# Two-layer backbone on one Trainium2 core: a PSUM copy held ahead of a weight cast in three feed-forward pairs, and one modulation dot instead of two before the token norm

## The chip, the cores and the metric

The program runs on one core of one Trainium2 chip. The metric is the device time of one execution in microseconds (us). The median of three runs of the kernel before is 1104.1 us, the lowest 1103.16, the highest 1105.3.

## What is computed

A residual stream of 512 latent tokens and 256 context tokens, 1024 features wide, passes through two layers. The first layer mixes tokens by latent attention and a short convolution, the second by a two-dimensional Fourier transform. Each layer ends in a SwiGLU feed-forward block. What the change touches is this block and the norm ahead of the Fourier transform:

```python
x = x + g1 * out_l
x = x + g2 * swiglu(rmsnorm(x, norm2_g[i]) * (1 + sc2) + sh2, ffn_w1[i], ffn_w3[i], ffn_w2[i])

def swiglu(h, w1, w3, w2):
    return (jax.nn.silu(h @ w1) * (h @ w3)) @ w2
```

The modulation vectors (`sh`, `sc`, `g`) come from `jax.nn.silu(c) @ ada_w[i] + ada_b[i]`, with 6144 outputs per layer.

## The kernel before, in words

**Arithmetic.** A product of 32-bit precision is made of three passes on TensorE (PE): each operand is split into a high and a low part, and high times high, low times high and high times low are added up in one PSUM bank. The split of a raw weight tile (128x1024) is one cast on ScalarE (ACT), whose name ends in `h`, and one subtraction on VectorE (DVE), whose name ends in `l` (`wsplit`, L151, and `split`, L142). Nearly every instruction is recorded at L92, the helper through which the engines are called, so it is followed by the names of its tiles.

**The feed-forward block.** `ffn` computes the up projections `h @ w1` and `h @ w3` for 22 blocks of 128 hidden features. The first 4 blocks of layer 0 and the first 6 of layer 1 are computed plainly (`up`); the others in pairs `p` of two blocks by a scheme with seven products instead of eight (`up_pair`, L1227). A product is 24 matmuls of 256 columns. Four PSUM banks belong to a pair: `ba`, `bb`, `be`, `bf`, in the trace `s_a`, `s_b`, `s_e`, `s_f`. The products come in this order:

- `11` into `ba`; then ACT copies `ba` into `bb` (L1258, in the trace `s_b<-s_a`);
- `s1` into `be`; then ACT copies `be` into an SBUF tile (L1261, in the trace `c<-s_e`);
- `s2`, added to `ba`, which may start when the copy `s_b<-s_a` has read `ba` and the weights `w_s2h` and `w_s2l` are split;
- `s4`, added to `be`; `s3`, added to `ba`; `12`, added to `bb`; `22`, added to `bf`.

Where the banks are still unused (`new`, L1234), a matmul of 512 columns first fills `bb` and `bf` (`fill_bank`). That is so in three pairs: pairs 2 and 3 of layer 0 and pair 3 of layer 1. After the pairs the down projection `w2` follows, whose weights are named `w_0` to `w_7`.

**Dots.** A modulation output is a dot of a row tile of `ada_w` with `silu(c)` on DVE (`dot`, L195; in the trace `junk<-ada,csil`, 128x1024). Dots are work in the background: `step(it, n)` emits the next `n` of them at chosen places. In layer 0 their row tiles have two buffers (`adap.tile(..., bufs=2)`, L1345), so the load of a row tile waits until the dot two places ahead of it has read its buffer.

**Order.** A scheduler orders each engine's instructions ahead of time, and each engine runs its list in that order. An instruction that passes through `tc.keep_in_program_order` keeps the program's order among the others that do; the dots do so, and the ones that `nc.ordered(True, ...)` covers. All loads are issued by SP, in one list too.

**The token norm.** Ahead of the Fourier transform, eight matmuls sum the squares of each token (`nm1st`), a short chain on DVE and ACT makes the reciprocal root (`rtok`), and four products `v` are scaled by it, split into `v1h` and `v1l` and go into the products `z`. Two dots are emitted ahead of that chain (L1426), and further ones between the splits (L1439).

Of the kernel before, what the change touches and what calls it, by code (L numbers as in the profile page):

```python
# [10 lines left out]
F32R = mybir.dt.float32r  # L11
# [6 lines left out]
P = 128  # L18
D = 1024
# [90 lines left out]
def backbone(ctx: ExitStack, tc: tile.TileContext, a, out):  # L110
    nc = Core(tc)
    PSUM = bass.MemoryType.PSUM

    def pool(name, bufs=1, side="left"):
        return tc.alloc_tile_pool(name=name, bufs=bufs, side=side, reuse_waits="tile")
# [10 lines left out]
    def ps2(name):  # L126
        return ps["pool"].tile([P, 2, 512], F32, tag="s2", name=name, bufs=3)
# [6 lines left out]
    def load(src, name, slots=None):  # L134
        t = slots(name) if slots else rawp.tile([P, src.shape[1]], F32, tag="raw", name=name)
        nc.sync.dma_start(out=t, in_=src)
        return t

    def f(ap):
        return ap.bitcast(F32)  # L140

    def split(hi, lo, src, eng=None):  # L142
        nc.scalar.copy(hi, src)
        (eng or nc.vector).tensor_sub(lo, src, f(hi))
# [6 lines left out]
    def wsplit(wpool, src, name, r_=None, eng=None):  # L151
        if r_ is None:
            r_ = load(src, name)
        n = r_.shape[1]
        hi = wpool.tile([P, n], F32R, tag="whi", name=name + "h")
        lo = wpool.tile([P, n], F32R, tag="wlo", name=name + "l")
        split(hi, lo, r_, eng)
        return hi, lo

    def step(it, n=1):  # L160
        for _ in range(n):
            next(it, None)
# [50 lines left out]
    def ada_chunk(l, chunk, by_pool=False, slots=None):  # L213

        m, sums = chunk * 8, []
        for i in range(8):
            w = load(a["ada"][l, m + i], f"ada{l}_{m + i}", slots)
            if by_pool:
                for n, _ in enumerate(dot_pool(w, csil)):
                    if n == LAG and sums:  # L220
                        total(*sums.pop())
                    yield
                sums.append((mod[:, l, m + i:m + i + 1], w))
            else:
                dot(mod[:, l, m + i:m + i + 1], w, csil)
                yield
        if sums:
            total(*sums.pop())
        nc.vector.tensor_add(mod[:, l, m:m + 8], mod[:, l, m:m + 8], col(C_AB + 48 * l + m, 8))
        if chunk in (1, 4):  # L230
            which = 0 if chunk == 1 else 1
            scale_cols(amod[:, l, which, :], mod[:, l, m:m + 8], col((C_N1, C_N2)[which] + 8 * l, 8))
# [249 lines left out]
    for n, k in enumerate(order):  # L482
# [20 lines left out]
        wh, wl = qw[k]  # L503
# [22 lines left out]
    def gain_split(src, g, hi, lo):  # L526
        nc.scalar.activation(hi, src, AF.Identity, scale=g)
        nc.vector.scalar_tensor_tensor(lo, src, g, f(hi), op0=ALU.mult, op1=ALU.subtract)
# [13 lines left out]
    def weight():  # L542

        taken.append(stream[len(taken)])
        return taken[-1]
# [85 lines left out]
    for c in range(3):  # L631
        w = weight()
# [147 lines left out]
    pin = tc.keep_in_program_order  # L780
# [169 lines left out]
    for i in range(NI - 3):  # L950
        h, t = divmod(i, 4)
# [60 lines left out]
    ring = pool("ring", RING, side="right")  # L1012
# [14 lines left out]
    def bank(o, i, t0, t1):  # L1027

        if t1 - t0 == T:
            return o[:, i, :]  # L1030
        return o[t0 // (t1 - t0)][:, 0, i * (t1 - t0):(i + 1) * (t1 - t0)]
# [120 lines left out]
    def cell(name):  # L1152

        return gfn.tile([P, 4, HT], F32, tag="c", name=name, bufs=4)

    def gate(sl, up_, hi, lo):

        if up_ is not None:
            nc.vector.tensor_mul(sl, up_, sl)
        split(hi, lo, sl)  # L1160
# [37 lines left out]
    def ffn(l, nf_, after, filler, nfill, first=None, first_out=lambda: None):  # L1198
# [28 lines left out]
        def up_pair(p, bank, g_):  # L1227

            def got(b):
                return load(a["wu"][l, p, b], f"wu{l}_{p}_{b}")  # L1230

            x_, y_, w_, z_ = (got(b) for b in range(4))
            bb, bf, ba, be = (bank(f"s{l}_{p}_{nm}") for nm in "bfae")
            new = len(used) <= 8  # L1234

            def fill_bank(o):

                if new:
                    nc.tensor.matmul(o, hh[:, KT - 1, 0:P], hh[:, KT - 1, :], start=True, stop=True)

            cf = gfn.tile([P, 2, 2, HT], F32, tag="c", name=f"c{l}_{p}", bufs=4)
            quads = [cf[:, i].rearrange("p w n -> p (w n)") for i in range(2)]

            def product(o, raw, block, start):

                wh, wl = wsplit(ring, None, f"w{l}_{p}_{block}", raw)
                rh, rl = bl[block]
                for i in range(2):
                    for k in range(4):
                        s = slice((4 * i + k) * P, (4 * i + k + 1) * P)  # L1250
                        d = o[:, i * HT:(i + 1) * HT]
                        for n, (wv, rv) in enumerate(((wh, rh), (wh, rl), (wl, rh))):
                            nc.tensor.matmul(d, wv[:, s], rv[:, k, :], start=start and i == k == n == 0,
                                             stop=(i == 1 and k == 3 and n == 2), skip_group_check=True)

            product(ba, x_, "11", True)
            fill_bank(bb)
            nc.scalar.copy(bb, ba)  # L1258
            nc.vector.tensor_sub(x_, y_, x_)
            product(be, x_, "s1", True)  # L1260
            nc.scalar.copy(quads[1], be)  # L1261
            nc.vector.tensor_sub(x_, w_, x_)
            product(ba, x_, "s2", False)
            fill_bank(bf)
            nc.scalar.copy(quads[0], ba)
            product(be, w_, "s4", False)
            nc.vector.tensor_add(quads[0], be, quads[0])
            nc.vector.tensor_sub(y_, w_, y_)
            product(ba, y_, "s3", False)
            nc.scalar.copy(bf, ba)  # L1270
            nc.vector.tensor_add(quads[1], ba, quads[1])
            product(bb, z_, "12", False)
            nc.vector.tensor_sub(x_, z_, x_)
            product(bf, x_, "22", False)
            gs = [[w[:, (2 * p + j) % 8, :].rearrange("p (i n) -> p i n", i=2) for w in g_] for j in range(2)]
            sl, up_ = cf[:, :, 0, :], cf[:, :, 1, :]
            nc.scalar.activation(sl, sl, AF.Silu)
            gate(sl, up_, *gs[1])
            sl = cell(f"sl{l}_{p}")[:, 0:2, :]
            for i, o in enumerate((bb, bf)):  # L1280
                nc.scalar.activation(sl[:, i, :], o[:, 0:HT], AF.Silu)
                nc.vector.tensor_mul(sl[:, i, :], o[:, HT:T], sl[:, i, :])
            gate(sl, None, *gs[0])
# [7 lines left out]
        for c, (c0, c1) in enumerate(CHUNKS):  # L1291
# [23 lines left out]
            for p in range(max(c0, NSTD[l]) // 2, c1 // 2):  # L1315
                up_pair(p, bank8, g_)
                step(it, nfill[0][c])
# [79 lines left out]
    def first(o, t, gs):  # L1397
        s = slice(t * P, (t + 1) * P)
        for g in gs:
            for j in range(2):  # L1400
                mm3(o[:, g // 2, (g % 2) * 256:(g % 2) * 256 + 256], [gained[nm][:, 2 * g + j, s] for nm in ("hi", "lo")],
                    (dft[0][:, j, :], dft[1][:, j, :]), j == 0, j == 1)
# [20 lines left out]
        first(v1_ps[t], t, range(3))  # L1423
    rtok = small("rtok", 4)
    late_dots = ada_chunk(1, 5, slots=lambda nm: cell(nm).rearrange("p k n -> p (k n)"))
    step(late_dots, 2)  # L1426
    nc.ordered(True, "vector", "scalar")
    gained["sums"].mean(0, T, D, rtok)
    rsqrt(rtok, rtok, 4, "rtok")
    for t in range(4):  # L1430
        if t < 2:
            first(v1_ps[t], t, (3,))
            o = v1_ps[t]
        else:
            o = ps2(f"v1_{t}")
            first(o, t, range(4))
        ov = o.rearrange("p two n -> p (two n)")
        gain_split(ov, rtok[:, t:t + 1], v1h[:, t].rearrange("p g c -> p (g c)"), v1l[:, t].rearrange("p g c -> p (g c)"))
        step(late_dots, (0, 0, 1, 2)[t])  # L1439
    wn = rawp.tile([4, D], F32, tag="raw", name="wn")  # L1440
    nc.sync.dma_start(out=wn, in_=a["wnyq"])
    wnh, wnl = (ring1.tile([P, D], F32R, tag=tag, name=f"wn_{tag}")[0:4] for tag in ("whi", "wlo"))
# [4 lines left out]
    for j in range(9):  # L1447
# [4 lines left out]
        for t in range(4):  # L1452
            if j == 8:
                w = (v1h[:, t, :, 128], v1l[:, t, :, 128])
            else:
                c0 = 0 if j < 4 else 128
                w = (v1h[:, t, j % 4, c0:c0 + 128], v1l[:, t, j % 4, c0:c0 + 128])
            mm3(zo, w, (tab[0][:, t, :], tab[1][:, t, :]), t == 0, t == 3 and tab is st_)
        for i in range(0 if tab is st_ else 2):
            if j < 4:  # L1460
                w = [w[:, i, 0:128] for w in dft], [w[:, 2 * j + i, :] for w in (pairs_h, pairs_l)]
            else:
                w = [w[:, i:KT:2, 0] for w in (pairs_h, pairs_l)], [w[:, KT + i, :] for w in (pairs_h, pairs_l)]
# [43 lines left out]
    for m in range(KT):  # L1507
# [4 lines left out]
        wh, wl = wfs[m]  # L1512
# [186 lines left out]
```

## Time and profile before

| | |
|---|---|
| median of 3 runs | 1104.1 us (1103.16 to 1105.3) |
| the profiled execution | 1105.53 us, of it 1103.5 us span |
| mean granted TensorE clock | 0.989 |
| PE busy | 97% of the span |
| DVE, ACT, POOL busy | 80%, 48%, 13% |

The span reaches from the first to the last instruction; some 2 us of the execution lie around it. Times of single instructions count from the span's start. PE is busy nearly throughout, so what matters are the few places in which it waits. [...]

### The profile page before, as it was taken

The page shows a single profiled execution, that of the slowest core. Times are in us where ns is not written, and L with a number is a line of the kernel's source. Part 1 is how long each engine was busy: PE and PEld are TensorE (multiplying, and loading weights), DVE is VectorE, ACT ScalarE, POOL GpSimd, SP SyncE. Part 2 cuts the span into 40 slices and gives each one's busy share as a digit, 9 for nine tenths or more (in the row PEclk, how much of TensorE's full clock was granted, in tenths as well). Part 3 has the DMA queues.
Part 4 walks back from the last instruction along what each step waited for, and adds up shares of the span by engine and source line. Part 5 has one row for each costly group of instructions (what it writes and reads, how often), then busy time and mean ns, then how long its engine had stood idle before and what let it go on. Part 6 is the DMA issues. An engine that isn't in the chain of part 4 may idle for free.

```text
span 1103.5 us, 17128 instructions
## 1 busy us (share of the span) xinstructions
PE 1066.9 (97%) x6704; PEld 950.2 (86%) x6704; DVE 877.4 (80%) x1282; ACT 528.6 (48%) x826; POOL 144.9 (13%) x160
## 2 busy tenths in 40 slices
PE   8799998999989999999999999999999999999998
PEld 7577886888888898899989988988888899989997
DVE  6988869998789897889678989898895577745862
ACT  5354456988445452256415564363543155523540
POOL 3811237775000000000000000011000000000000
PEclk8999999999999999999999999998999999999999
DMA  7778640111661357643674573313334124422231
GB/s 257 248 277 293 216 154 17 39 39 39 229 211 58 122 191 260 206 156 116 190 221 142 162 269 134 114 41 108 122 92 157 39 96 134 134 96 73 71 96 67
DMA packets 45528, 156.95 MB, mean 142 GB/s; under 512 B 5252, under 2 KB 6276, under 8 KB 45320
## 3 DMA queue, kind: packets, MB, share of 16 engines
q1 hardware_dynamic: 45448, 155.87, 43.2%
q8 instruction: 52, 0.85, 0.3%
q14 instruction: 28, 0.23, 0.1%
HBM read 153.75 MB, written 2.10 MB: 141 GB/s over the span
## 4 chain that ended last, share of the span: by engine, by line
PE 78%; DVE 15%; ACT 3%; issue 3%; DMA 1%; POOL 1%; SPq 0%; ACTq 0%; DVEq 0%; POOLq 0%
PE f L92 24%; PE s_a L92 12%; PE s_e L92 8%; PE s_f L92 4%; PE s_b L92 4%; PE s_ps L92 4%; PE o L92 3%; DVE junk L92 2%; PE t_ps L92 2%; PE pv_ps L92 2%; PE ob L92 2%; PE fo L92 2%; PE ou L92 2%; PE oc L92 1%; PE f_third L92 1%
## 5 line engine op out<-in xcount | busy, mean ns | idle before, releaser
L92 DVE SCALAR_TENSOR_TENSOR junk<-ada,csil 128x1024 bf16<-128x1024 f32 x88 | 113.3, 1288 | 14.6 <-DMA ada<-in_ada 13.9
L92 DVE SCALAR_TENSOR_TENSOR x<-f,mod,x 128x512 f32<-128x512 f32 (+1 forms) x50 | 36.4, 728 | 65.2 <-PE f L92 65.1
L92 DVE TENSOR_TENSOR wu<-wu,wu 128x1024 f32<-128x1024 f32 x68 | 83.1, 1222 | 1.2
L92 POOL TENSOR_TENSOR w<-w,mod 128x1024 f32<-128x1024 f32 x4 | 7.9, 1972 | 474.9 <-DVE w_0l L92 456.1
L92 PE MATMUL s_a<-sh,w_s2h 128*128 128x256 f32 x136 | 39.1, 288 | 2.3 <-ACT s_b L92 2.3
L92 PE MATMUL s_a<-sh,w_s2l 128*128 128x256 f32 x136 | 39.2, 288 | 0.1
L92 PE MATMUL s_a<-sl,w_s2h 128*128 128x256 f32 x136 | 39.0, 287 | 0.0
L92 PE MATMUL s_e<-sh,w_s1l 128*128 128x256 f32 x136 | 38.4, 283 | 0.0
L92 PE MATMUL s_e<-sh,w_s1h 128*128 128x256 f32 x136 | 38.4, 282 | 0.0
L92 PE MATMUL s_e<-sl,w_s1h 128*128 128x256 f32 x136 | 38.4, 282 | 0.0
L92 PE MATMUL s_a<-sh,w_s3l 128*128 128x256 f32 x136 | 38.4, 282 | 0.0
L92 PE MATMUL s_a<-sh,w_s3h 128*128 128x256 f32 x136 | 38.3, 282 | 0.0
L92 PE MATMUL s_a<-sl,w_s3h 128*128 128x256 f32 x136 | 38.3, 282 | 0.0
L92 ACT CAST w_11h<-wu 128x1024 fp32r<-128x1024 f32 x17 | 17.8, 1050 | 41.4 <-PE f L92 18.0
L92 DVE TENSOR_TENSOR w_22l<-wu,w_22h 128x1024 fp32r<-128x1024 f32 x17 | 20.8, 1225 | 20.1 <-ACT w_22h L92 20.1
L92 ACT CAST w_s2h<-wu 128x1024 fp32r<-128x1024 f32 x17 | 17.8, 1050 | 39.4 <-DVE wu L92 26.8
L92 DVE TENSOR_TENSOR ptl<-t_ps,pth 128x384 fp32r<-128x384 f32 x62 | 31.4, 547 | 3.2 <-ACT pth L92 3.0
L92 POOL TENSOR_SCALAR p<-p,m 128x768 f32<-128x768 f32 x32 | 29.0, 908 | 24.1 <-DVE m L92 20.9
L92 DVE TENSOR_REDUCE m<-s_ps 128x1 f32<-128x768 f32 x32 | 30.3, 948 | 0.6 <-PE s_ps L92 0.5
L92 ACT CAST w_s1h<-wu 128x1024 fp32r<-128x1024 f32 x17 | 17.9, 1051 | 26.8 <-DVE wu L92 17.2
L92 ACT ACTIVATE p<-s_ps,m 128x768 f32<-128x768 f32 x32 | 29.2, 913 | 0.8 <-DVE m L92 0.8
L92 ACT CAST pth<-t_ps 128x384 fp32r<-128x384 f32 x62 | 26.6, 479 | 5.5 <-PE t_ps L92 5.1
(1011 smaller groups left out, 4161.9 us busy)
## 6 DMA issues: line engine op xcount, KB each, us to landing
ada<-in_ada SPq DMA_DIRECT2D x96, 512.0 KB, 4.5
wu<-in_wu SPq DMA_DIRECT2D x68, 512.0 KB, 4.1
w<-in_w SPq DMA_DIRECT2D x52, 512.0 KB, 4.3
adac<-in_ada SPq DMA_DIRECT2D x16, 512.0 KB, 5.8
wc<-in_wconv SPq DMA_DIRECT2D x12, 512.0 KB, 5.1
w<-in_w SPq DMA_DIRECT2D x16, 384.0 KB, 3.8
wo<-in_wo SPq DMA_DIRECT2D x8, 512.0 KB, 4.2
wf<-in_wf SPq DMA_DIRECT2D x8, 512.0 KB, 4.4
```

The source lines that it names most:

```text
L92: ins = fn(*args, **kw)
```

## The change

In the three pairs whose banks are new, the copy `s_b<-s_a` and the cast that makes `w_s2h` are both kept in program order, so that the scheduler may no longer put the cast ahead of the copy. To that end the split of a product's weights is written out. Ahead of the token norm one dot is emitted instead of two; the other is emitted behind the second `v1l`.

```diff
+            pin = False
+
+            def keep(ins):
+                return tc.keep_in_program_order(ins) if pin else ins
+
             def product(o, raw, block, start):
 
-                wh, wl = wsplit(ring, None, f"w{l}_{p}_{block}", raw)
+                wh = ring.tile([P, D], F32R, tag="whi", name=f"w{l}_{p}_{block}h")
+                wl = ring.tile([P, D], F32R, tag="wlo", name=f"w{l}_{p}_{block}l")
+                keep(nc.scalar.copy(wh, raw))
+                nc.vector.tensor_sub(wl, raw, f(wh))
                 rh, rl = bl[block]
...
             product(ba, x_, "11", True)
             fill_bank(bb)
-            nc.scalar.copy(bb, ba)
+            pin = new
+            keep(nc.scalar.copy(bb, ba))
             nc.vector.tensor_sub(x_, y_, x_)
+            pin = False
             product(be, x_, "s1", True)
             nc.scalar.copy(quads[1], be)
             nc.vector.tensor_sub(x_, w_, x_)
+            pin = new
             product(ba, x_, "s2", False)
+            pin = False
...
-    step(late_dots, 2)
+    step(late_dots)
...
-        step(late_dots, (0, 0, 1, 2)[t])
+        step(late_dots, (0, 1, 1, 2)[t])
```

The first place is ACT's list in pair 2 of layer 0 (`w_2` and `s_2` are that pair's weights and banks, `f_3`, `sl_3`, `gh_0` belong to the block before it). Rows with a minus stand in the order before, rows with a plus in the new one.

```order
 L92 CAST nf0hi<-u_s_3513 128x4x256
+L92 ACTIVATE sl_3_3670<-f_3_0_3618 128x512
+L92 CAST gh_0_3313<-sl_3_3670 128x512
+L92 COPY s_2_b<-s_2_a 128x512
+L92 COPY c_2_3694<-s_2_e 128x512
 L92 CAST w_2_s2h<-wu_2_0_3682 128x1024
-L92 ACTIVATE sl_3_3670<-f_3_0_3618 128x512
 L92 CAST w_2_s4h<-wu_2_2_3686 128x1024
-L92 CAST gh_0_3313<-sl_3_3670 128x512
 L92 CAST w_2_s3h<-wu_2_1_3684 128x1024
-L92 COPY s_2_b<-s_2_a 128x512
 L92 CAST w_2_12h<-wu_2_3_3688 128x1024
```

Not only the copy `s_b<-s_a` but also the copy `c<-s_e` now stands ahead of the cast of `w_s2h`; the casts of `w_s4h` and `w_s3h` stand behind it as before. In pair 3 of layer 0 and pair 3 of layer 1 the two copies and the casts stand in the same order.

The second place is DVE's list in pair 3 of layer 0, where three dots stood between the low parts of the weights (`w_3_s2l` and so on); `ada_42` to `ada_45` are the row tiles of the dots.

```order
 L92 TENSOR_TENSOR gl_0_3314<-sl_2_3907,gh_0_3313 128x512
 L92 SCALAR_TENSOR_TENSOR junk,mod<-ada_42_3914,csil 128x1024
+L92 SCALAR_TENSOR_TENSOR junk,mod<-ada_43_3917,csil 128x1024
+L92 SCALAR_TENSOR_TENSOR junk,mod<-ada_44_3920,csil 128x1024
+L92 TENSOR_TENSOR w_3_s2l<-wu_3_0_3926,w_3_s2h 128x1024
+L92 SCALAR_TENSOR_TENSOR junk,mod<-ada_45_3923,csil 128x1024
+L92 TENSOR_TENSOR w_3_s4l<-wu_3_2_3930,w_3_s4h 128x1024
 L92 TENSOR_TENSOR w_3_s3l<-wu_3_1_3928,w_3_s3h 128x1024
-L92 SCALAR_TENSOR_TENSOR junk,mod<-ada_43_3917,csil 128x1024
```

`w_3_s2l` and `w_3_s4l`, which stood ahead of the dot of `ada_42`, now stand behind the dots of `ada_44` and `ada_45`.

The third place is DVE's list at the token norm (`nm1st` are the summed squares).

```order
 L92 SCALAR_TENSOR_TENSOR amod<-mod,cols 128x8
 L92 SCALAR_TENSOR_TENSOR junk,mod<-ada_40_6769,csil 128x1024
-L92 SCALAR_TENSOR_TENSOR junk,mod<-ada_41_6772,csil 128x1024
-L92 TENSOR_SCALAR rtok<-nm1st_6775 128x4
+L92 TENSOR_SCALAR rtok<-nm1st_6772 128x4
 L92 RECIPROCAL rtoks<-rtoks 128x4
```

The dot of `ada_41` leaves its place ahead of `rtok`; it now stands between the second and the third `v1l`.

## Rows read from the trace of the kernel before

**Rows 1.** The page: busy time, share of the span and count of each engine.

```profile
PE 1066.9 (97%) x6704; PEld 950.2 (86%) x6704; DVE 877.4 (80%) x1282; ACT 528.6 (48%) x826; POOL 144.9 (13%) x160
```

**Rows 2.** Busy time by windows: length, busy time (instructions) by engine, granted clock, DMA share, GB/s.

```profile
354.00:687.00 333.00, 332.01 (x2211) 303.24 (x2211) 284.80 (x367) 148.45 (x200) 0.00 (x0) 1.00 0.56 180
```

**Rows 3.** Timeline of PE, pair 3 of layer 1: start, duration, instruction, idle before.

```profile
820.27 0.28 PE L92 MATMUL s_e<-sh,w_s1l 128*128 128x256 f32 x1
822.83 0.39 PE L92 MATMUL s_a<-sh,w_s2h 128*128 128x256 f32 x1 [2.27 <-ACT s_b L92]
...
827.54 0.28 PE L92 MATMUL s_e<-nf1hi,w_s4h 128*128 128x256 f32 x1
...
830.26 0.28 PE L92 MATMUL s_a<-sh,w_s3h 128*128 128x256 f32 x1
```

**Rows 4.** Timeline of ACT, pair 3 of layer 1.

```profile
818.84 1.05 ACT L92 CAST w_s2h<-wu 128x1024 fp32r<-128x1024 f32 x1 [3.25 <-DVE wu L92]
...
822.20 0.58 ACT L92 COPY s_b<-s_a 128x512 f32<-128x512 f32 x1
```

**Rows 5.** Busy time by windows, token norm and pair 3 of layer 1.

```profile
686.00:690.00 4.00, 1.86 (x13) 1.56 (x13) 2.69 (x5) 3.13 (x3) 0.00 (x0) 1.00 0.53 210
820.60:822.80 2.20, 0.00 (x0) 0.00 (x0) 2.20 (x4) 2.20 (x5) 0.00 (x0) 1.00 0.00 0
...
824.10:827.50 3.40, 3.40 (x17) 3.37 (x16) 2.19 (x2) 0.43 (x2) 0.00 (x0) 0.50 0.67 211
827.60:830.00 2.40, 2.40 (x23) 2.40 (x22) 1.23 (x1) 1.14 (x2) 0.00 (x0) 1.00 0.76 266
```

**Rows 6.** Timeline of ACT, pair 2 of layer 0.

```profile
373.65 1.05 ACT L92 CAST w_s2h<-wu 128x1024 fp32r<-128x1024 f32 x1 [3.62 <-PE f L92]
...
380.44 1.05 ACT L92 CAST w_12h<-wu 128x1024 fp32r<-128x1024 f32 x1 [1.56 <-issue]
381.40 0.58 ACT L92 COPY c<-s_e 128x512 f32<-128x512 f32 x1
```

**Rows 7.** Timeline of PE, pairs 2 and 3 of layer 0.

```profile
380.19 0.28 PE L92 MATMUL s_e<-sh,w_s1l 128*128 128x256 f32 x1
...
383.43 0.28 PE L92 MATMUL s_e<-nf0hi,w_s4h 128*128 128x256 f32 x1
...
386.15 0.29 PE L92 MATMUL s_a<-sh,w_s3h 128*128 128x256 f32 x1
...
400.59 0.29 PE L92 MATMUL s_a<-sh,w_s2h 128*128 128x256 f32 x1
...
406.42 0.29 PE L92 MATMUL s_a<-sh,w_s3h 128*128 128x256 f32 x1
```

**Rows 8.** Timeline of DVE, pairs 2 and 3 of layer 0.

```profile
374.73 1.23 DVE L92 TENSOR_TENSOR w_s2l<-wu,w_s2h 128x1024 fp32r<-128x1024 f32 x1 [2.11 <-ACT w_s2h L92]
...
386.42 0.69 DVE L92 TENSOR_TENSOR c<-s_e,c 128x512 f32<-128x512 f32 x1 [0.79 <-PE s_e L92]
...
399.28 1.22 DVE L92 SCALAR_TENSOR_TENSOR junk<-ada,csil 128x1024 bf16<-128x1024 f32 x1
...
405.27 1.23 DVE L92 SCALAR_TENSOR_TENSOR junk<-ada,csil 128x1024 bf16<-128x1024 f32 x1 [0.20 <-DMA ada<-in_ada]
```

**Rows 9.** Timeline of SP's list, pair 3 of layer 0: issues of loads.

```profile
400.54 0.33 SPq L136 DMA_DIRECT2D ada<-in_ada  x1
```

**Rows 10.** All 96 loads of `ada` tiles on SP's list, from issue to landing.

```profile
DMA to landing us min/median/max: 3.3/4.5/8.7
```

**Rows 11.** Timeline of DVE at the token norm.

```profile
684.06 1.22 DVE L92 SCALAR_TENSOR_TENSOR junk<-ada,csil 128x1024 bf16<-128x1024 f32 x1
...
685.21 0.16 DVE L92 TENSOR_SCALAR rtok<-nm1st 128x4 f32<-128x4 f32 x1
```

**Rows 12.** Timeline of PE at the token norm.

```profile
687.67 0.39 PE L92 MATMUL z<-tab_sh,v1h 128*128 128x258 f32 x1 [1.57 <-ACT v1h L92]
...
688.99 0.39 PE L92 MATMUL v<-tab_sh,nm1hi 128*128 128x256 f32 x1 [0.57 <-DVE v1l L92]
```

## The prediction

> **What bounds the kernel now.** I read the busy shares first: PE is busy for 97% of the span, the next engine (DVE) for 80% [rows 1]. So the kernel is a chain of matmuls, and a change pays or costs where PE waits. A row of windows then shows how few waits there are in the part in question: from the last plain block of layer 0 to the token norm PE is busy for 332.01 of 333.00 us [rows 2]. Two conclusions follow. The two layer-0 pairs that the change touches have no wait to remove. And a wait that is put there is not made good later: nothing behind it is idle that could take it up.
>
> The timeline of PE shows the waits at the other two places. In pair 3 of layer 1 the last matmul of `s1` starts at 820.27 and the first of `s2` at 822.83, after 2.27 us idle, ended by the copy `s_b<-s_a` [rows 3]. ACT shows why: it cast `w_s2h` at 818.84 and three more tiles before it came to the copy at 822.20 [rows 4]. [...] At the token norm PE waits 1.57 us and a little later 0.57 [rows 12].
>
> **The change part by part.**
>
> *Order on ACT.* The change asks for the copy ahead of the cast of `w_s2h`. The new order puts the copy `c<-s_e` ahead of it as well, and that copy reads the bank that `s1` writes; it cannot start before `s1` ends. So the weights of `s2`, which before were cast some 6 us ahead (373.65, against the end of `s1` at 380.47 [rows 6, 7]), now begin to be made when PE already wants them. From the end of `s1` the path is: copy 0.58 (the next instruction on ACT starts about 0.09 before the end of the one ahead: 380.44 + 1.05 against 381.40), cast 1.05 [rows 6], low part on DVE 1.23, which starts 0.03 after the cast ends [rows 8], and 0.1 for three handovers: 0.04 + 0.49 + 1.05 + 0.03 + 1.23 + 0.05 = 2.9 us. PE is not wholly idle in this time: the new order gives it the fill of `bf` and two matmuls each of `s2` and `s4`. What is left for PE then is 22 matmuls of `s2` and 22 of `s4`. Before, 24 of `s4` took 386.15 - 383.43 = 2.72, and `s2` with the fill (as long as two) took 383.43 - 380.31 = 3.12, so 0.12 each [rows 7]; `s2` started 0.12 after the last matmul of `s1`. 22 and 22 make 2.64 + 2.49 = 5.1.
>
> *Pair 2 of layer 0.* `s1` ends at 380.47; +2.9 is 383.4; +5.1 is 388.5, against 386.15, where `s3` started before [rows 7]. **+2.4 us.** Below 2.1 it can't go: that would need the three steps of the path to be shorter than their rows. The weights of `s3` and after are made while PE works on `s2` and `s4`, and stay ahead.
>
> *Pair 3 of layer 0.* Here DVE comes on top. `w_s2l` now stands behind the dots of `ada_42`, `ada_43` and `ada_44`, and the tile of `ada_44` is loaded into the buffer that the dot of `ada_42` frees. In the trace before, that dot ran at 399.28, SP issued the load at 400.54, and the dot of `ada_44` could start at 405.27, ended by the load [rows 8, 9]: 4.7 us after the buffer was free. It hurt nobody then, since `w_s2l` and `w_s4l` had gone ahead. When does the dot of `ada_42` run now? DVE's sum `c<-s_e` of pair 2 ran at 386.42 and comes 2.4 later, 388.8. From there to the dot took 12.9 us of nearly full DVE work; two low parts leave this stretch (2 x 1.2) and one enters (`w_22l`, which stood ahead): 11.6 at most, less what DVE waited in it. I take 400.2 for the dot, 401.5 for the issue, 406.2 for the dot of `ada_44`, 407.4 for `w_s2l`, 408.6 for PE. 5.1 later is 413.7, against 406.42 [rows 7]: +7.3, of which 2.4 came from pair 2. **+4.9 us.** The dot of `ada_45` and `w_s4l` end near 411, just when PE is through with `s2`; half a microsecond may be lost there. The bounds come from the load: the 96 loads of such tiles take 3.3 to 8.7, median 4.5 [rows 10], which makes +3.5 to about +9.
>
> *The clock in pair 3.* Its wait is some 4.6 us but for four matmuls, twice the 2.27 that brought the clock down in layer 1 [rows 3, 5]. So I charge one fall, **+1.6 us**; bounds 0 and two falls, 3.2.
>
> *Pair 3 of layer 1.* The 2.27 wait for `s_b<-s_a` goes, but the same path as in layer 0 takes its place: `s1` ends at 820.55, +2.9 is 823.5, +5.1 is 828.6, if the clock stays at 1.00. Before, `s3` started at 830.26 [rows 3]. **-1.7 us**, or 0 if the clock falls as before. So a stall is exchanged for one about as long, and what is won is only its fall of the clock.
>
> *Token norm.* One dot of 1.22 leaves the path to `rtok` [rows 11], PE's 1.57 wait behind it shrinks by as much [rows 12], and the 0.57 wait moves along. The dot returns ahead of the third `v1l`, which then is ready no earlier than before, and some of the gain may be lost there. **-1.0 us**, bounds 0 and -1.6. All else (the split written out, the order of `z`) issues the same instructions.
>
> **Sum:** 2.4 + 4.9 + 1.6 - 1.7 - 1.0 = +6.2 us. The profiled execution took 1105.53 (span 1103.5), so the sum gives 1111.7 for one like it; it lay 1.4 above the median of the runs. On the median it is 1104.1 + 6.2 = **1110.3 us**. About 0.2% (2.2 us) is what a measurement of this kernel can tell from no change.
>
> **The rivals.**
>
> *The clock falls in the other two pairs too.* In the forecast pair 2 of layer 0 and pair 3 of layer 1 keep it. Their waits are about 1.4 and 0.6 us with two matmuls between; the nearest row, 1.57 and 0.57 with four between, kept 1.00 [rows 5, 12], but 2.27 in one piece did not. Each fall adds 1.6: 1111.9 with one, 1113.5 with both. [...]
>
> *The load of `ada_44` lands in time.* Then pair 3 costs 2.3 like pair 2 and its clock stays: 2.4 + 2.3 - 1.7 - 1.0 = +2.0, that is 1106.1: not slower by what can be told. It decides at 404.7, where the cast of `w_s2h` ends; the tile would have to land by 403.4, some 2 us after its buffer is free. Against it: no load took under 3.3 [rows 10]. For it: only that DVE may reach the first dot earlier than I count.
>
> *The copy doesn't hold the cast,* because it need not wait for the whole of `s1`. Then pair 2 loses nothing, and in layer 1 `s2` follows `s1` at once: `s3` at 820.43 + 3.12 + 2.72 = 826.2, 4.1 ahead of before. The dots in pair 3 still stand in the way: `w_s2l` comes 2.4 earlier than I count, PE at 406.2, `s3` at 411.3, +4.9. Sum 4.9 - 4.1 - 1.0 = -0.2: 1103.9, no change, or 1105.5 with a fall of the clock in pair 3. Against it: `c<-s_e` started at 381.40, after the end of `s1` at 380.47 [rows 6, 7]. Only this and the load in time together make it faster: 1099.
>
> *More is late in pair 3:* a slow load, or `w_s4l` later than `s2` ends: 1 to 4 us more, 1111 to 1114 and, with another fall of the clock, 1115.
>
> **How the numbers follow.** Forecast 0.53; more falls of the clock 0.28; more late in pair 3 0.07; load in time 0.06; copy not in the way 0.04; both of these 0.02. Low end: the forecast with a load of 3.3 (-1.4), no fall in pair 3 (-1.6) and a little more from the norm (-0.3): 1107.0. High end: both further falls and a load that is 1.5 late: 1115.0. This leaves out the last three cases and the tails. Slower by over 0.2% takes the first three: 0.88; within 0.2% the load in time and the copy: 0.10; faster both: 0.02.
>
> **What would show it.** In the timeline of ACT the cast of `w_s2h` starts right behind `c<-s_e`, about 0.5 us after the end of `s1`, in all three pairs. On PE the third matmul of `s2` waits for `w_s2l`, in pair 3 of layer 0 for 2 us and more, with the dot of `ada_44` ended by its load just ahead. The clock is 0.50 for a stretch after that. In layer 1 the wait for `s_b` is gone. At the token norm PE waits about 0.4 us for `v1h`. I am wrong if PE runs on from `s1` to `s2` in layer 0, or if the stretch between those pairs and the token norm turns out shorter than before by what the pairs lost.

## The result, and the profile after

The changed kernel took **1114.95 us** (median of 4 runs, 1114.27 to 1115.49); the kernel before, run beside it, 1104.70 (4 runs, 1103.16 to 1108.28). The ratio is **1.0094, 95% interval 1.0072 to 1.0115**: slower, as forecast, but by some 10 us where the sum was 6.2. A second set of runs (`after_again`, below) gave 1.0069, 1.0055 to 1.0083, which is 8 us. Beside the experiments the kernel before ran 74 times more (1101.4 to 1108.88), in three sets with medians of 1105.2, 1106.2 and 1105.9, so the base of 1104.1 on which the forecast stood was 1 to 2 us low.

The profiled execution of the change took 1115.09 us (span 1113.2), that of before 1105.53 (span 1103.5): +9.6. First the page of the change: the busy times and the two groups of PE that wait.

```profile
PE 1072.7 (96%) x6704; PEld 953.5 (86%) x6704; DVE 877.0 (79%) x1282; ACT 528.7 (47%) x826; POOL 144.5 (13%) x160
...
L92 PE MATMUL s_a<-sh,w_s2h 128*128 128x256 f32 x136 | 40.3, 296 | 4.3 <-ACT w_s2h L92 4.3
L92 PE MATMUL s_a<-sh,w_s2l 128*128 128x256 f32 x136 | 40.5, 298 | 1.1 <-DVE w_s2l L92 1.1
```

PE is busy for 5.8 us more than before [rows 1] with as many instructions: matmuls ran longer, at a mean granted clock of 0.983 against 0.989. And it waits 4.3 us for `w_s2h`, three waits of some 1.4, one for each pair that the change touches. The means on the page say the same of `s2`: its matmuls with `sh` and `w_s2h` took 296 ns on average, those of `s3` with `w_s3h` 282.

To find where the time went I compared the starts of the same matmuls, the last of `s1` and the first of `s3`, in both traces. Timeline of PE of the change; in square brackets stands the idle time just before a matmul, and what ended it:

```profile
382.70 0.28 PE L92 MATMUL s_e<-sh,w_s1l 128*128 128x256 f32 x1
384.66 0.39 PE L92 MATMUL s_a<-sh,w_s2h 128*128 128x256 f32 x1 [1.44 <-ACT w_s2h L92]
385.60 0.39 PE L92 MATMUL s_e<-nf0hi,w_s4h 128*128 128x256 f32 x1 [0.44 <-ACT w_s4h L92]
385.95 0.42 PE L92 MATMUL s_a<-sh,w_s2l 128*128 128x256 f32 x1
...
392.66 0.28 PE L92 MATMUL s_a<-sh,w_s3h 128*128 128x256 f32 x1
...
406.98 0.28 PE L92 MATMUL s_e<-sh,w_s1l 128*128 128x256 f32 x1
408.88 0.39 PE L92 MATMUL s_a<-sh,w_s2h 128*128 128x256 f32 x1 [1.39 <-ACT w_s2h L92]
409.82 0.46 PE L92 MATMUL s_e<-nf0hi,w_s4h 128*128 128x256 f32 x1 [0.44 <-ACT w_s4h L92]
411.62 0.58 PE L92 MATMUL s_a<-sh,w_s2l 128*128 128x256 f32 x1 [1.11 <-DVE w_s2l L92]
...
419.16 0.28 PE L92 MATMUL s_a<-sh,w_s3h 128*128 128x256 f32 x1
...
833.60 0.39 PE L92 MATMUL s_a<-sh,w_s2h 128*128 128x256 f32 x1 [1.45 <-ACT w_s2h L92]
834.54 0.39 PE L92 MATMUL s_e<-nf1hi,w_s4h 128*128 128x256 f32 x1 [0.44 <-ACT w_s4h L92]
...
840.10 0.28 PE L92 MATMUL s_a<-sh,w_s3h 128*128 128x256 f32 x1
```

One line more of pair 3 before, beside [rows 7]:

```profile
400.47 0.28 PE L92 MATMUL s_e<-sh,w_s1l 128*128 128x256 f32 x1
```

The three first matmuls of `s3` stand 6.51, 12.74 and 9.84 us behind those of before [rows 7, 3]. What a pair costs is read here and below from the last matmul of `s1` to the first of `s3`: 9.96 us in pair 2 and 12.18 in pair 3, against 5.96 and 5.95 before. Going through the span, the shift between the two profiles grows like this:

| stretch | shift gained, us | of it |
|---|---|---|
| up to pair 2 of layer 0 | +2.5 | clock low for longer near 178 us, and low near 355 us |
| pair 2 of layer 0 | +4.0 | stall 2.5, clock 1.5 |
| pair 3 of layer 0 | +6.2 | stall 3.8, clock 2.4 |
| on to the token norm | -0.6 | |
| token norm | -0.8 | |
| pair 3 of layer 1 | -1.5 | no fall of the clock here |

The granted clock, as a share of full speed (the number ahead of the last two), by windows of the change:

```profile
382.20:385.95 3.75, 1.87 (x13) 1.32 (x11) 1.31 (x2) 2.87 (x4) 0.00 (x0) 1.00 0.28 107
385.95:389.30 3.35, 3.35 (x18) 3.35 (x17) 3.35 (x4) 1.50 (x2) 0.00 (x0) 0.52 0.38 86
...
409.85:416.60 6.75, 5.64 (x25) 5.34 (x26) 6.75 (x9) 1.81 (x2) 0.00 (x0) 0.51 0.68 202
```

Read them as in [rows 5]: in pair 2 PE works 1.87 of 3.75 us at 1.00, then 3.35 us at 0.52. In pair 3 the clock stays down twice as long, 6.75 us at 0.51, of which PE idles 1.1. What that cost is seen from the first matmul with `w_s2l` to the first of `s3`: 6.71 us in pair 2 and 7.54 in pair 3, against 5.18 (386.39 to 391.57) in the run below whose clock stayed up there. So the clock cost 1.5 and 2.4, and the rest of each pair's loss is stall.

Why pair 3 waits longer, by the timeline of DVE of the change:

```profile
404.37 1.22 DVE L92 SCALAR_TENSOR_TENSOR junk<-ada,csil 128x1024 bf16<-128x1024 f32 x1
...
409.19 1.23 DVE L92 SCALAR_TENSOR_TENSOR junk<-ada,csil 128x1024 bf16<-128x1024 f32 x1 [2.33 <-DMA ada<-in_ada]
...
410.34 1.22 DVE L92 TENSOR_TENSOR w_s2l<-wu,w_s2h 128x1024 fp32r<-128x1024 f32 x1
```

The dot of `ada_42` runs at 404.37 and that of `ada_44` waits 2.33 us for its load, with `w_s2l` behind it. That is the step of the prediction; SP issued the load at 405.62, so it took 3.6 to the start of the dot, not the 4.7 of before [rows 8, 9]. The other step stands on ACT, here in pair 2, where the cast comes right behind `c<-s_e`:

```profile
383.08 0.59 ACT L92 COPY c<-s_e 128x512 f32<-128x512 f32 x1 [2.34 <-PE s_e L92]
383.56 1.05 ACT L92 CAST w_s2h<-wu 128x1024 fp32r<-128x1024 f32 x1
```

The token norm, timeline of PE:

```profile
698.70 0.39 PE L92 MATMUL z<-tab_sh,v1h 128*128 128x258 f32 x1 [0.40 <-ACT v1h L92]
700.02 0.39 PE L92 MATMUL v<-tab_sh,nm1hi 128*128 128x256 f32 x1 [0.57 <-DVE v1l L92]
...
719.74 0.39 PE L92 MATMUL fo<-z_hl,wf0h 128*128 128x258 f32 x1 [0.27 <-DVE z_hl L92]
```

The wait of 1.57 shrinks to 0.40, the 0.57 stays [rows 12], and a wait of 0.27 a little later is new.

One thing in the table is no part of the change: the clock near 178 and 355 us. From 174.3 to 181.1 us it is 0.51 here and 0.75 before: a fall in both, longer here. Ahead of 355 both kernels wait alike (for `w_3h` 1.19 and 0.21 or 0.22, for `w_2l` 0.50 or 0.51), yet the clock of 355.2 to 358.6 is 1.00 in the trace before, with 16 matmuls, and 0.53 in this one, with 9. Before, then the change:

```profile
355.20:358.60 3.40, 3.40 (x16) 2.73 (x16) 3.40 (x4) 1.06 (x1) 0.00 (x0) 1.00 0.37 140
355.20:358.60 3.40, 3.40 (x9) 2.66 (x10) 3.40 (x4) 0.72 (x2) 0.00 (x0) 0.53 0.57 149
```

Over the thirteen profiles of this case a fall stands near 355 us in two, near 330 in six, among them two whose kernels are as before up to there, and near neither in five. So the 2.5 of the 9.6 between these two executions that arose ahead of the changed pairs is chance, as far as these profiles tell, and such falls are a part of why runs of one kernel differ by several us: of the 28 runs of the kernel before in the last of the three sets, the fastest, 1102.07 us, has a mean clock of 0.992, the slowest, 1108.42, one of 0.984. Each experiment is therefore read twice: by its median, and by the shift in its profile at the place in question.

A word on the mechanism, which the text on the order told too loosely: the order listings fit the reading that an instruction which passes through `tc.keep_in_program_order` is held behind whichever instruction the program issued just ahead of it on its engine. For the cast of `w_s2h` that is `c<-s_e`, not `s_b<-s_a`. So the change says one copy and holds the cast behind another, later one.

### The profile page after: what moved, and what is told of

Its sections match the earlier page's. It is cut to its first block, busy times and chain, and to the rows that moved or that the text cites. A ratio compares the mean times of both kernels' runs of the same rounds, so it can differ in the third digit from the quotient of the medians.

```text
span 1113.2 us, 17119 instructions
## 1 busy us (share of the span) xinstructions
PE 1072.7 (96%) x6704; PEld 953.5 (86%) x6704; DVE 877.0 (79%) x1282; ACT 528.7 (47%) x826; POOL 144.5 (13%) x160
## 4 chain that ended last, share of the span: by engine, by line
PE 77%; DVE 16%; ACT 3%; issue 3%; DMA 1%; POOL 1%; SPq 0%; DVEq 0%; ACTq 0%; POOLq 0%
PE f L92 23%; PE s_a L92 13%; PE s_e L92 8%; PE s_b L92 4%; PE s_f L92 4%; PE s_ps L92 4%; DVE junk L92 3%; PE o L92 3%; PE t_ps L92 2%; PE pv_ps L92 2%; PE ob L92 2%; PE f_third L92 2%; PE fo L92 2%; PE ou L92 1%; PE oc L92 1%
## 5 line engine op out<-in xcount | busy, mean ns | idle before, releaser
L92 PEld LDWEIGHTS s_a<-sh,w_s2h 128*128 128x128 f32 x136 | 27.4, 201 | 5.2 <-ACT w_s2h L92 5.2
L92 DVE TENSOR_TENSOR w_s2l<-wu,w_s2h 128x1024 fp32r<-128x1024 f32 x17 | 20.8, 1225 | 11.5 <-ACT w_s2h L92 11.2
```

The costliest lines, as they stand in the source:

```text
L92: ins = fn(*args, **kw)
```

## The experiments

My theory: the loss lies in the two layer-0 pairs alone, is made by `c<-s_e` ahead of the cast, and is three costs on top of each other: the stall, the load of `ada_44` in pair 3, and the falls of the clock. The rivals: the copy `s_b<-s_a` itself makes it; the layer-1 pair or the norm has a part; the clock costs nothing beside the waits.

### The norm alone

```diff
-    step(late_dots, 2)
+    step(late_dots)
...
-        step(late_dots, (0, 0, 1, 2)[t])
+        step(late_dots, (0, 1, 1, 2)[t])
```

> The kernel before with one dot instead of two ahead of the token norm, and nothing else. If the parts add up: PE's wait for v1h goes from 1.57 to about 0.4 us and the time falls by 0.9 to 1.2 us, to about 1103.5. If the dot that comes back behind the second v1l takes the gain away: no change. On the clock: if the falls at 178 to 185 us and at 355 to 359 us, which the changed kernel's profile had and the one of before had not (1.2 and 1.6 us), come with the changed pairs, they are absent here; if they are a matter of when a run starts, either may be here too.

Measured: 1104.69 us (12 runs, 1101.73 to 1107.11), ratio 0.9992 (0.9977 to 1.0007). In the profile PE reaches the `z` products 1.1 to 1.2 earlier against its neighbours and loses 0.35 at `fo`: some -0.8. So the term is there, but by itself too small to be told from nothing in the time.

### The order held in layer 0 alone

```diff
-            pin = new
+            pin = new and l == 0
```

(at both places)

> The changed kernel with the pins in layer 0 alone; pair 3 of layer 1 is as before. Order theory (the two layer-0 pairs make the loss, the layer-1 pair gives 1.6 back): 1.6 us slower than the changed kernel, 1116 to 1117, with PE's 2.27 us wait for s_b back in layer 1. If layer 1 gave nothing or lost: 1113 to 1115.

Measured: 1115.37 us (6 runs, 1113.57 to 1116.77), ratio 1.0087 (1.0066 to 1.0107), the whole loss of the change. The 1.6 that it was expected to lie above the change can't be told: it lies 0.4 to 1.2 above the two medians. The profile has pair 2 at +4.0 and pair 3 at +6.2, with the clock low in the same two places, and PE's wait of 2.27 for `s_b` is back in layer 1, with the fall behind it.

### The order held in layer 1 alone

```diff
-            pin = new
+            pin = new and l == 1
```

> The changed kernel with the order held in layer 1 alone; layer 0 as before, the norm as in the change. By the order theory both layer-0 terms go, with their clock falls, and layer 1 (0 to -1.7) and the norm (about -0.9) are left: 1102.5 to 1104.5. If the loss of the change comes from anything else than the two layer-0 pairs, it stays above 1107.

Measured: 1105.37 us (12 runs, 1103.07 to 1107.45), ratio 0.9997 (0.9985 to 1.0010). The loss is gone, which is what the order theory says; the gain stays at the small end, and the median lies 0.9 above the range that I gave, with a base that was higher too. In its profile layer 1 gains 1.5 and the norm 0.8.

### The same copy, with `c<-s_e` behind the cast

```diff
+            early = new and PINS[l]
+            if not early:
+                nc.scalar.copy(bb, ba)
...
+            if early:
+                nc.vector.tensor_sub(x_, w_, x_)
+                nc.scalar.copy(bb, ba)
+                pin = True
+                ready = weights(x_, "s2")
+                pin = False
+                nc.scalar.copy(quads[1], be)
...
+            product(ba, x_, "s2", False, ready)
```

(`weights` is the split of `product`, by itself; both `PINS` are true, so the copy is written just ahead of the cast that is held in all three pairs)

> All three pairs keep the copy s_b<-s_a ahead of the cast of w_s2h, but the copy c<-s_e is no longer ahead of it: s_b is traced just ahead of the cast, c<-s_e behind. Token norm as in the change. Theory that c<-s_e ahead of the cast makes the stalls: layer 0 loses nothing, PE runs on from s1 to s2 in pair 2, layer 1 as in the changed kernel or a little better: 1101 to 1104. Rival, that holding s_b ahead of the cast is what costs: 1112 to 1116, with PE waiting for w_s2l in both layer-0 pairs.

Measured: 1105.68 us (12 runs, 1100.79 to 1107.77), ratio 0.9997 (0.9981 to 1.0013): far from the rival's 1112 and more, and 1.7 above my own range. Timeline of ACT, pair 2 of layer 0:

```profile
376.56 0.57 ACT L93 COPY s_b<-s_a 128x512 f32<-128x512 f32 x1 [1.64 <-PE s_b L93]
377.04 1.05 ACT L93 CAST w_s2h<-wu 128x1024 fp32r<-128x1024 f32 x1
...
379.89 0.59 ACT L93 COPY c<-s_e 128x512 f32<-128x512 f32 x1
```

The copy that the change names stands ahead of the cast here too, and costs nothing in pair 2: the cast starts at 377.04, while `s1` runs. Pair 3 costs 0.5, after a wait of 0.27 for `w_s2l`. From 354 to 687 us PE is busy for 331.80 of 333, nearly as before [rows 2]. So it is `c<-s_e` that costs. What missed my range is in part the norm, which gave nothing in this profile: PE's wait for `v1h` fell to 0.36, but one of 1.19 for `z_hl` came at `fo`.

### The change once more

> The changed kernel once more, to see which clock falls come back. If the two waits in layer 0 bring the clock down by themselves, a fall stands again right behind s2 of pair 2 and again behind s2 of pair 3, while those near 178 and 355 us, where the change touches nothing, need not be there: 1113 to 1116 us. If the falls in the two pairs were chance, one or both are missing and the median of more runs is 1110 to 1112.

Measured: 1114.18 us (5 runs, 1111.89 to 1115.20), ratio 1.0069 (1.0055 to 1.0083). The clock is low again in `s2` of pair 2 and for twice as long in pair 3, and in layer 1 too this time (after waits of 1.45 and 0.44, the same as above, where it held):

```profile
385.40:388.80 3.40, 3.40 (x18) 3.40 (x18) 3.40 (x4) 1.39 (x2) 0.00 (x0) 0.50 0.37 98
409.30:416.10 6.80, 5.78 (x26) 5.49 (x27) 6.80 (x9) 1.83 (x3) 0.00 (x0) 0.50 0.68 200
832.50:835.90 3.40, 3.40 (x18) 3.40 (x18) 3.40 (x4) 1.30 (x2) 0.00 (x0) 0.51 0.39 107
```

So the falls in the layer-0 pairs belong to the change, that in layer 1 comes and goes. Over all eight profiles that have the change's order in layer 1, the clock fell there in three.

### The dots out of the way

```diff
-                step(it, nfill[0][c])
+                step(it, (2, 6)[p - 2] if l == 0 and c == 0 else nfill[0][c])
```

> The changed kernel with the dots of ada_44 and ada_45 taken out from ahead of w_3_s2l and w_3_s4l in pair 3 of layer 0; the order on ScalarE is as in the changed kernel. If pair 3 pays for the load of ada_44 (the prediction's step), its stall falls from about 3.8 to about 2.4, as in pair 2, and with it perhaps one window of the clock: 1.5 to 3 us less than the changed kernel, 1112 to 1113.5. If the copy c<-s_e alone makes the stall, nothing changes: 1114 to 1116.

Measured: 1114.42 us (5 runs, 1111.83 to 1115.65), ratio 1.0073 (1.0059 to 1.0087): by the median nothing, as the rival had it. The profiled execution was the fastest of the five; in it DVE's wait ahead of `w_s2l` is ended by the cast and no longer by a load, pair 3 costs 3.9 instead of 6.2, and the clock is low once in each pair (DVE, then windows of pair 2 and pair 3):

```profile
408.34 1.23 DVE L92 TENSOR_TENSOR w_s2l<-wu,w_s2h 128x1024 fp32r<-128x1024 f32 x1 [1.99 <-ACT w_s2h L92]
```

```profile
385.40:388.80 3.40, 3.40 (x18) 3.38 (x17) 3.40 (x4) 1.54 (x2) 0.00 (x0) 0.50 0.36 93
409.30:412.70 3.40, 3.39 (x16) 3.39 (x17) 3.40 (x4) 1.85 (x2) 0.00 (x0) 0.50 0.43 105
```

The expected 1.5 to 3 are in the profile and not in the median. The mean clock of the other four runs is 0.981 to 0.983 against 0.986 here, so they spent more time at the low clock, but where can't be seen without a trace of them.

### PE kept busy in the wait

```diff
-            fill_bank(bf)
+            for _ in range(7 if new and l == 0 else 1):
+                fill_bank(bf)
```

> The changed kernel with seven instead of one fill of the bank bf in each of the two layer-0 pairs; they stand between s1 and s2 on TensorE, write zeros and need no weights, so TensorE is busy for about 1.4 us more of each wait and the wait itself stays. If the granted clock is a cost of its own, the falls behind pair 2 (1.5) and behind pair 3 (1.5 to 3) go or get fewer: 1110 to 1112.5. If the clock costs nothing beside the waits, or the fills don't keep it up: 1114.5 to 1116.5.

Measured: 1113.95 us (6 runs, 1109.99 to 1115.35), ratio 1.0061 (1.0044 to 1.0079): 0.2 less than `after_again`, below what can be told, and between the two ranges that I had given. The fills don't write zeros, as was said above, but the product that the one fill wrote before; each overwrites the last. The windows of pair 2 show what they were put there for, and the timeline of PE the time from `s1` to `s3`:

```profile
382.00:385.10 3.10, 3.03 (x20) 2.40 (x18) 0.01 (x1) 1.58 (x3) 0.00 (x0) 1.00 0.46 163
385.10:389.00 3.90, 3.45 (x26) 3.23 (x27) 3.90 (x4) 2.80 (x3) 0.00 (x0) 1.00 0.15 23
```

```profile
383.15 0.28 PE L92 MATMUL s_e<-sh,w_s1l 128*128 128x256 f32 x1
...
386.39 0.36 PE L92 MATMUL s_a<-sh,w_s2l 128*128 128x256 f32 x1
...
391.57 0.28 PE L92 MATMUL s_a<-sh,w_s3h 128*128 128x256 f32 x1
```

The clock stays at 1.00 through `s2`, and pair 2 costs 2.5 instead of 4.0. In pair 3 PE still waits 1.42 for `w_s2l`, which waits for the load, and the clock still falls, once; the pair costs 5.6. This execution, the slowest of its six, has more low clock elsewhere than that of before: falls near 35 and 355 us, and a longer one near 178. So the gain is in the profile of pair 2 and not in the median.

### Both edits together

The edits of the last two sections in one kernel.

> The changed kernel with both edits in layer 0: the dots of ada_44 and ada_45 later, and seven fills of bf instead of one in each wait. If stalls and clock falls add as the profiles of the two single edits say (dots about -2.2 in pair 3, fills about -1.5 in pair 2 and up to -1.5 in pair 3), what is left in layer 0 is two stalls of about 2.4 and no fall: 1108.5 to 1111. If the medians of the single edits are right and neither pays: 1113 to 1115.

Measured: **1108.12 us** (11 runs, 1106.38 to 1110.45), ratio 1.0020 (1.0007 to 1.0033): against `after_again` 5 to 6 us of the loss are gone, with the order on ACT still that of the change. Windows of PE, then the last matmul of `s1` and the first of `s3` in both pairs:

```profile
382.20:385.50 3.30, 2.78 (x20) 2.39 (x20) 3.07 (x3) 3.03 (x4) 0.00 (x0) 1.00 0.03 7
385.50:388.50 3.00, 3.00 (x28) 3.00 (x27) 2.69 (x3) 0.81 (x2) 0.00 (x0) 1.00 0.91 262
404.00:408.00 4.00, 3.53 (x24) 2.81 (x23) 3.09 (x3) 3.72 (x4) 0.00 (x0) 1.00 0.57 212
408.00:414.00 6.00, 6.00 (x52) 6.00 (x52) 4.91 (x6) 2.59 (x3) 0.00 (x0) 1.00 0.80 262
```

```profile
380.49 0.28 PE L92 MATMUL s_e<-sh,w_s1l 128*128 128x256 f32 x1
...
389.01 0.28 PE L92 MATMUL s_a<-sh,w_s3h 128*128 128x256 f32 x1
...
403.03 0.28 PE L92 MATMUL s_e<-sh,w_s1l 128*128 128x256 f32 x1
...
411.50 0.28 PE L92 MATMUL s_a<-sh,w_s3h 128*128 128x256 f32 x1
```

The clock is 1.00 throughout. From `s1` to `s3` it takes 8.52 and 8.47 us, against 5.96 and 5.95 before, so the pairs cost 2.6 and 2.5. That is the bare stall, close to what the prediction had (2.4, and 2.3 without the load). The rest of the change's loss in layer 0, 5.1 of 10.2, is the load and the clock.

Why does each edit alone show so little in the median? In windows that no edge of a fall cuts, the clock was 1.00 or 0.50 (in the change 1.00 from 377 to 382.2 us, 0.50 from 176 to 180). If it has no third value, a run's span and its mean granted clock give the time it spent at 0.50, to about 1 us. The median of that time is 33.4 us in `after_again`, 40.1 with the dots alone, 33.4 with the fills alone and 24.3 with both; before, it is 26.5 to 28.7 in the three sets. If low clock costs about half its length (1.5 of 3.4 us in pair 2 of the change), the runs with the dots alone lost 3 us to it, enough to hide the 1.4 of stall that pair 3 gained, and both edits together won 4 to 5 from the clock and over 1 from the load. Why the runs with the dots alone spent more time at the low clock is not shown.

### One pair of layer 0 at a time

```diff
-            pin = new
+            pin = new and (l == 1 or p == 2)
```

> The changed kernel with the order held in pair 2 of layer 0 and in layer 1, not in pair 3 of layer 0. By the sum of terms pair 2 costs 2.4 of stall and 1.5 of clock, layer 1 and the norm give back 0.9 to 2.5: 1106.5 to 1108.5, between before and change; the profile shows pair 3 without a wait. If the loss needs both pairs (DVE late in pair 3 only because pair 2 was late) it is all the same 3.9 here, so that only a time above 1110 speaks against the sum.

Measured: 1109.86 us (11 runs, 1108.70 to 1112.24), ratio 1.0037 (1.0024 to 1.0049), 1.4 above my range. Pair 2 costs 4.0 in the profile, and pair 3 waits for nothing. The clock in pair 2:

```profile
384.50:388.00 3.50, 3.50 (x17) 3.50 (x18) 3.50 (x5) 1.71 (x2) 0.00 (x0) 0.51 0.31 66
```

Further on, behind the token norm, the clock of this execution is low from 702 to 709 us, which gives some 2.6 more.

The same with `p == 3`:

> The changed kernel with the order held in pair 3 of layer 0 and in layer 1, not in pair 2. If the load of ada_44 and the dots ahead of w_3_s2l make pair 3 dear by themselves: a stall of 3 to 4 and one or two falls, 6 in all, less 0.9 to 2.5 for layer 1 and norm: 1108.5 to 1110.5. If pair 3 is dear only because pair 2 had made DVE late, it costs what pair 2 costs (3.9): 1106.5 to 1108.5.

Measured: 1108.66 us (12 runs, 1105.59 to 1113.37), ratio 1.0027 (1.0012 to 1.0042), just inside the range of the first theory. The profile has 4.8 for pair 3; timeline of DVE, then the clock:

```profile
402.51 1.23 DVE L92 SCALAR_TENSOR_TENSOR junk<-ada,csil 128x1024 bf16<-128x1024 f32 x1 [2.61 <-DMA ada<-in_ada]
...
403.66 1.22 DVE L92 TENSOR_TENSOR w_s2l<-wu,w_s2h 128x1024 fp32r<-128x1024 f32 x1
```

```profile
404.40:407.80 3.40, 2.87 (x13) 2.87 (x14) 3.40 (x5) 1.02 (x2) 0.00 (x0) 0.50 0.77 193
```

The load is waited for although nothing ahead was late, so pair 3 is dearer than pair 2 by itself; behind a late pair 2 it cost 6.2, with the clock low for twice as long. By the ratios the two pairs add: 4.1 and 3.0 us above before, less the -0.3 of layer 1 and norm alone that both contain, make 7.4; the change itself had 7.6 and 10.4 in its two sets.

### A version that beats both

From the same finding: in layer 1 the cast isn't what keeps PE waiting in the kernel before, it is the casts ahead of the copy `s_b<-s_a` [rows 4]. So layer 0 is left as it was, and in pair 3 of layer 1 the copy goes first, then the cast of `w_s2h`, then the cast `gh` of the block before, which is put off to that place.

```diff
-                gate(sl, os_[j][1], g_[0][:, j % 8, :], g_[1][:, j % 8, :])
+                args = (sl, os_[j][1], g_[0][:, j % 8, :], g_[1][:, j % 8, :])
+                if defer:
+                    kept.append(args)
+                else:
+                    gate(*args)
...
+            if early:
+                nc.vector.tensor_sub(x_, w_, x_)
+                nc.scalar.copy(bb, ba)
+                pin = True
+                ready = weights(x_, "s2")
+                pin = False
+                while kept:
+                    g_sl, g_up, g_hi, g_lo = kept.pop()
+                    nc.vector.tensor_mul(g_sl, g_up, g_sl)
+                    tc.keep_in_program_order(nc.scalar.copy(g_hi, g_sl))
+                    nc.vector.tensor_sub(g_lo, g_sl, f(g_hi))
+                nc.scalar.copy(quads[1], be)
```

> Layer 0 as before; in layer 1 the copy s_b<-s_a stands ahead of the cast of w_s2h and both ahead of the cast gh of the block before, which waits for DVE; c<-s_e is behind. Token norm as in the change. Order theory: s_b runs in ACT's idle time near 817.5, PE waits under 0.7 us for w_s2l in place of 2.27 and the clock does not fall there: 3.3 to 4.1 us less in layer 1, 1.0 at the norm, together 1099 to 1100.5. If ACT's or DVE's other work is what holds s2 in layer 1: 1102 to 1104.

(`PINS` is false for layer 0 and true for layer 1.)

Measured: **1102.04 us** (12 runs, 1099.66 to 1103.89), ratio **0.9966 (0.9952 to 0.9980)**: faster than before by 3 to 4 us (2 to 5 by the interval), though 1.5 above the expected range and in that of the rival. Timeline of PE and window of pair 3 of layer 1, then PE behind the token norm:

```profile
819.12 0.39 PE L93 MATMUL s_a<-sh,w_s2l 128*128 128x256 f32 x1 [0.49 <-DVE w_s2l L93]
```

```profile
812.00:826.00 14.00, 13.51 (x112) 13.11 (x111) 13.40 (x13) 9.58 (x12) 0.00 (x0) 1.00 0.25 71
```

```profile
707.88 0.39 PE L93 MATMUL fo<-z_hl,wf0h 128*128 128x258 f32 x1 [1.01 <-DVE z_hl L93]
```

The wait of 2.27 [rows 3] is 0.49 here, and the clock does not fall; in the profile layer 1 gains 3.3, as the order theory has it. The 1.0 of the norm is what is missing: PE's wait for `v1h` is 1.0 shorter, and 1.01 comes back as a wait for `z_hl` at `fo`.

## Why the prediction was right and wrong

**Right:** the direction, the place and what makes the waits. PE waits for `w_s2h` in all three pairs, the cast stands right behind `c<-s_e` (383.08 and 383.56 on ACT in pair 2), `w_s2l` of pair 3 stands behind the load of `ada_44`. The bare stalls came out nearly as worked: 2.4 forecast for pair 2, 2.5 and 2.6 measured where the clock was kept up; 2.3 for pair 3 without the load, 2.5 measured. One sign came only in part: PE was to wait at the third matmul of `s2` for `w_s2l`, in pair 3 for 2 us and more; it waits for `w_s2h` (1.4) and `w_s4h` (0.44) in each pair, and for `w_s2l` only in pair 3, for 1.11. The time lies inside the range, at its very top: two of the four runs are above it.

**Wrong: the term of the clock.** The step that failed is the sentence on the rivals that "In the forecast pair 2 of layer 0 and pair 3 of layer 1 keep it", with its reason, that waits of 1.57 and 0.57 at the token norm had kept 1.00. Pair 2, after waits of 1.44 or 1.45 and 0.44, had a low clock in all five profiles that have its wait without fills, at 1.5 each; with the waits filled it fell in neither of two. One fall was charged for layer 0; the change paid 1.5 in pair 2 and 2.4 in pair 3, together 3.9 instead of 1.6. The rival that has more falls had been given 0.28. A single row that kept its clock was no evidence for another place: the pair of rows at 355 us has 1.00 behind the same waits in one execution and 0.53 in the other. The size of one fall was a little off too. The sum's 1.6 is the difference of two windows of [rows 5]: 17 matmuls take 3.40 us at 0.50, and as 23 take 2.40 at 1.00, 17 were put at 1.77. But a window's count takes in matmuls cut by its edges; at the 0.12 from start to start of [rows 7] 17 take 2.0, so that fall cost 1.4. So no run shows the 1.6 itself: they showed this 1.4, and the 1.5 of pair 2.

**Pair 3's stall** was forecast at 4.9 and measured 3.8 in the change: the load took 3.6 us, not 4.7, and PE itself came later. With the clock term of 2.4 the pair cost 6.2 against a forecast of 4.9 + 1.6 = 6.5, so here an error was covered by another; that the pair as a whole fits is luck.

**Layer 1 and the norm.** Forecast -1.7 and -1.0; the profile of the change has -1.5 and -0.8. But the -1.7 needs the clock to hold, which it did in five of eight profiles, and the timed kernel that has these terms alone gave -0.3 (-1.7 to +1.1). The norm's gain is not safe either: its 1.2 at `v1h` was followed by a wait for `z_hl` at `fo` that was 0.2 to 0.4 us in six profiles (0.27 in the change) and 0.9 to 1.2 in five, which takes nearly all of it; in the twelfth the clock is low there. That the gain might be lost was in the prediction's bounds, at another place. So on average these terms gave less than the one profile says.

**The base.** 1104.1 was the median of three runs; the three later sets put it 1 to 2 us higher.

Summed up by what was measured: 4.0 + 6.2 for the pairs, some -0.9 for layer 1 (-1.5 in five of eight), 0 to -0.8 for the norm: +8.5 to +9.3, between the two ratios (7.6 and 10.4).

## What to carry to other kernels

Look at what an ordering primitive is really tied to: here "the copy ahead of the cast" was tied to the instruction issued last on that engine, another copy that came a whole product later, and the order listing showed it before anything ran. Where PE is the bound and a change opens waits in it, give each new wait its own chance of a fall of the clock, not only the longest, and do not take one row that kept the clock as evidence for another place: behind waits of 1.4 and 0.44 us it fell in five of five profiles in pair 2 of layer 0 and in three of eight in layer 1. If a wait can't be removed, PE can be kept busy through it, as by the fills in pair 2, where the clock then was 1.00. And where single runs of a kernel scatter by several us, take the place from the profile and the sum from many runs: with 5 or 6, edits worth 1.5 to 2.3 in a profile did not show in the median.

## What the runs showed of the hardware that was not expected

The granted clock is part of the scatter: behind waits of 1.19, 0.21 and 0.51 us it was 1.00 in one execution and 0.53 in another, and 1.45 with 0.44 behind it in layer 1 was followed by both as well. A fall of 3.4 us cost 1.5 where PE had work throughout, and one of 6.75 us, with PE idle for 1.1 of it, 2.4. With six fills more, 1.4 us of work in the wait, the clock of pair 2 stayed at 1.00 in both profiles that have them.
